# An encoder trunk on one core: the split weight rows laid out without gaps, all at one place modulo 256 bytes from the activations

## The chip, the core and the metric

The kernel runs on one core of a Trainium2 chip. The number compared is the device time of one execution in microseconds (us), the median of several runs. A profiled execution gives the trace from which the rows below are taken. In it TensorE has two rows: PE are the matrix multiplications (MATMUL), PEld the loads of the stationary operand (LDWEIGHTS), one before each MATMUL, loaded while the MATMUL before it still streams. ACT is ScalarE, DVE is VectorE, SP issues most DMAs.

## The reference

A two-layer bidirectional encoder over 256 tokens of width 2048, in float32. Cut to what matters here, it is a row of matrix products with small work between them:

```python
def sq_relu_mlp(h, w1, w2):
    a = jax.nn.relu(h @ w1)
    return (a * a) @ w2

def reference(x, attn_norm, mlp_norm, w_mlp_in, w_mlp_out, even_w_in, even_rpb, even_w_out,
              odd_w_qkv, odd_sink, odd_w_out, final_norm):
    for i in range(DEPTH):
        h = rms_norm(x, attn_norm[i])
        j = i // 2
        if i % 2 == 0:
            x = x + even_mixer(h, even_w_in[j], even_rpb[j], even_w_out[j])
        else:
            x = x + odd_mixer(h, odd_w_qkv[j], odd_sink[j], odd_w_out[j])
        x = x + sq_relu_mlp(rms_norm(x, mlp_norm[i]), w_mlp_in[i], w_mlp_out[i])
    return rms_norm(x, final_norm)
```

`even_mixer` projects to 6144 columns of queries, keys and values, runs 8 heads of neighbourhood attention and 8 of dilated attention and projects back; `odd_mixer` projects to 3072 columns, runs 16 query heads on 4 key heads in a window, and projects back. The MLPs are 2048 to 8192 to 2048. All weights are read once, and the products with them are nearly all of the work.

## The kernel before

**Split products.** To keep float32 accuracy with the one-pass type float32r, each operand is a high part (the value rounded to float32r) and a low part (what the rounding left). A product is high times high, high times low and low times high. The activations lie as `[P, k, 2, T]`: for each group k of 128 input channels, 256 high values and then 256 low values per partition, in the tiles `u` (normed input), `o` (head outputs) and `hid` (MLP hidden layer). The weights come in units of 128 output columns, in halves of eight rows k, 128 x 128 values each. `load_halves` issues the DMA of a half from SP into `r`; `split` (L84, L85) makes the high part `h` on ACT and the low part `l` on DVE. Up to three halves are loaded ahead, from pools of five buffers (`whi`, `wlo`).

**The matrix products.** `k_range` (L155, L157) issues for each k two MATMULs: one with `h` as stationary operand and all 512 columns of the activation's high and low part streamed past it, and one with `l` as stationary operand and the 256 high columns streamed. This document calls these two a *dense pair*. There are 5,344 of them; in the very last unit L152 and L153 take the place of L155, and in the first stage L476 and L477 do the same work as the weights arrive. Pairs of the value projection are other: `value_products` (L276) has the activation `u` stationary and 256 columns of the weight streamed, three MATMULs per k and half of the tokens (`u` high with `h`, `u` high with `l`, `u` low with `h`), 960 in all. Attention adds scores (L312), transposes (L337) and value sums (L356).

**What sets the order.** The program is written out in the order of the units; small work of attention and norms is put between them by a step counter (`later`, `tick`). Each engine runs its own instructions in order.

**Where the operands lie.** In `before` a row of `h` or `l` takes `ROW = P + 8` values, 544 bytes, so that row k begins 32 bytes further modulo 256 than row k-1, and the rows of a half go once round all eight multiples of 32. `h` and `l` of one k lie alike. `u` begins at 128 modulo 256; `hid` and `o` begin at 32; the row of an activation is 2,048 bytes, so all its rows begin alike. The "difference" below is the address of the stationary operand minus that of the streamed one, in bytes modulo 256: in dense pairs it takes all eight multiples of 32 equally often, and every eighth pair has the same one. Weight tiles for the value projection are filled without gaps already, and there the difference between `u` and the streamed weight is 192 in every MATMUL (64 in the first stage, where the rows are 544 bytes apart). In L312 and L356 both operands begin at 32, difference 0.

Of the kernel before, what the change touches and what calls it, by code (L numbers as in the profile page):

```python
# [7 lines left out]
F32 = mybir.dt.float32  # L8
F32R = mybir.dt.float32r
# [5 lines left out]
P = 128  # L15
T = 256
# [8 lines left out]
SCALE = 128.0 ** -0.5  # L25
TW = 384
HALF = KT // 2
ROW = P + 8
RAW_BUFS = 6
LATE = 12  # L30
PART_BUFS = 5
# [11 lines left out]
def encoder(ctx: ExitStack, tc: tile.TileContext, a: dict, outT: bass.AP):  # L43
    nc = tc.nc

    const = ctx.enter_context(tc.tile_pool(name="const", bufs=1))
    raw = ctx.enter_context(tc.tile_pool(name="raw", bufs=RAW_BUFS))
    whi = ctx.enter_context(tc.tile_pool(name="whi", bufs=PART_BUFS))
    wlo = ctx.enter_context(tc.tile_pool(name="wlo", bufs=PART_BUFS))
    held_w = ctx.enter_context(tc.tile_pool(name="held_w", bufs=3))  # L50
    work = ctx.enter_context(tc.tile_pool(name="work", bufs=3))
# [16 lines left out]
    rb2 = const.tile([P, T], F32, name="rb2")  # L68
    rcol = const.tile([P, 2], F32, name="rcol")
    warmed = const.tile([P, 1], F32, name="warmed")  # L70
    gate = const.tile([P, 1], F32, name="gate")

    nc.scalar.dma_start(g, a["gains"])
    nc.vector.memset(ones, 1.0)
# [8 lines left out]
    def split(hi, lo, src):  # L83
        nc.scalar.activation(hi, src, AF.Copy)  # L84
        nc.vector.tensor_sub(lo, src, hi.bitcast(F32))  # L85
# [6 lines left out]
    def need(units, held=0, flat=False):  # L92

        for i, src in enumerate(units):
            pending.extend([(src[:, :HALF, :], HALF, flat),
                            (src[:, HALF:, :], HALF - 2 if i < held else HALF, flat)])

    def load_halves(n):
        while pending and len(loaded) < n:
            src, n, flat = pending.pop(0)  # L100
            r = raw.tile([P, HALF, P], F32, name="r")
            nc.sync.dma_start(r, src)
            h = whi.tile([P, HALF, ROW], F32R, name="h")
            l = wlo.tile([P, HALF, ROW], F32R, name="l")
            if flat:
                h, l = (w.rearrange("p k c -> p (k c)")[:, :HALF * P] for w in (h, l))
                split(h, l, r.rearrange("p k c -> p (k c)"))
                loaded.append((h, l, None))
                continue
            h, l = h[:, :, :P], l[:, :, :P]  # L110
            split(h[:, :n, :], l[:, :n, :], r[:, :n, :])
            tiles = [(h[:, k, :], l[:, k, :]) for k in range(n)]
            if n < HALF:
                h, l = (held_w.tile([P, 2, P], F32R, name=name) for name in ("hh", "hl"))
                split(h, l, r[:, n:, :])
                tiles += [(h[:, k, :], l[:, k, :]) for k in range(2)]
            loaded.append((h, l, tiles))

    def take_half():
        load_halves(AHEAD + 1)  # L120
        return loaded.pop(0)
# [20 lines left out]
    def finish_tasks():  # L142
        while tasks:
            now[0] = max(now[0], tasks[0][0])
            run_due()
# [44 lines left out]
    def gained(k, which, x=None):  # L190
        gk = g[:, which, k:k + 1]
        if x is None:
            x = xs[:, k, :]
        if which == 4:
            nc.scalar.activation(x, x, AF.Copy, scale=gk)
        else:
            nc.scalar.activation(u[:, k, 0, :], x, AF.Copy, scale=gk)
            nc.vector.scalar_tensor_tensor(u[:, k, 1, :], x, gk, u[:, k, 0, :].bitcast(F32),
                                           op0=ALU.mult, op1=ALU.subtract)

    def squares(k, x=None):
        if x is None:
            x = xs[:, k, :]
        if k == 0:
            nc.scalar.activation(ssq, x, AF.Square)
        else:
            sq = work.tile([P, T], F32, name="sq", bufs=2)
            nc.scalar.activation(sq, x, AF.Square)
            nc.vector.tensor_add(ssq, ssq, sq)
# [60 lines left out]
    def value_products(ps, k, h, l):  # L270

        for j in range(2):
            js = slice(j * P, (j + 1) * P)
            out = ps[:, j * T:(j + 1) * T].rearrange("p (a c) -> p a c", a=2)
            for n, (x, y) in enumerate(((0, h), (0, l), (1, h))):
                nc.tensor.matmul(out, u[:, k, x, js], y, start=k == 0 and j == 0 and n == 0,  # L276
                                 stop=k == KT - 1 and n == 2, skip_group_check=True)
# [181 lines left out]
    for k in range(KT):  # L459
        r = raw.tile([P, HALF, P], F32, name="r")  # L460
# [5 lines left out]
    for k in range(KT):  # L466
        r = packs[k]
        x = r[:, :2, :].rearrange("p a c -> p (a c)")
        gained(k, 0, x)
        h, l = (pool.tile([P, HALF, ROW], F32R, name=name)[:, :6, :P] for pool, name in ((whi, "h"), (wlo, "l")))  # L470
        split(h, l, r[:, 2:, :])
        squares(k, x)
        if k == LATE:
            nc.gpsimd.tensor_copy(gate, r[:, 0, 0:1])
        for i in range(4):
            nc.tensor.matmul(sps[i], h[:, i, :], u[:, k].rearrange("p a t -> p (a t)"), start=k == 0, stop=False)  # L476
            nc.tensor.matmul(sps[i][:, :T], l[:, i, :], u[:, k, 0, :], start=False, stop=k == KT - 1)  # L477
        value_products(vps, k, h[:, 4:, :], l[:, 4:, :])
# [5 lines left out]
    with tc.tile_pool(name="attn0", bufs=1) as pool:  # L484
# [25 lines left out]

        q, k, v = [[], []], [[], []], []
        load_halves(1)
        for i in range(2):
            for j, (dst, name, sc) in enumerate(((q, "q", SCALE), (k, "k", 1.0))):
                head_parts(pool, name, 2, sc, dst[i])(sps[2 * i + j])
            load_halves(2)
            attend(pool, o, i, q[i], k[i], v, i, bias_of(i), (LAGS_0[0] + 4 * i,) + LAGS_0[1:])
        norm["waiting"].append(lambda v=v: keep_values(pool, v, vps))
        for p in range(1, 8):
# [6 lines left out]
            q, k, v = [[], []], [[], []], []  # L526
            for i in range(2):
                for j, (dst, name, sc) in enumerate(((q, "q", SCALE), (k, "k", 1.0))):
                    unit(head_parts(pool, name, 2, sc, dst[i]), u)
                h = 2 * p + i  # L530
# [7 lines left out]
    with tc.tile_pool(name="attn1", bufs=1) as pool:  # L538
        o = pool.tile([P, NH, 2, T], F32R, name="o")
        sl = slopes(16)  # L540
        for p in range(2):
            k, v = [[], []], []
# [8 lines left out]
            for i in range(8):  # L551
                h = 8 * p + i
# [3 lines left out]
                       LAGS_1 if h < NH - 3 else LAGS_END, True)  # L556
        project_out(o, 3)
        finish_tasks()
    last_sq = work.tile([P, T], F32, name="last_sq", bufs=1)

    def last_added(ps):
        y = work.tile([P, T], F32, name="y", bufs=1)
# [96 lines left out]
```

## Time and profile before

| | |
|---|---|
| time, median of 3 runs | 2103.64 us (2103.43 to 2104.03) |
| the profiled execution | 2105.7 us, span 2103.8 us |
| granted TensorE clock, mean | 0.996 |
| PE busy | 2086.0 us, 99% of the span |
| DVE busy | 1340.9 us, 64% |
| ACT busy | 1035.6 us, 49% |
| DMA | mean 185 GB/s |

How to read it: a MATMUL's busy time overlaps that of the next (a 512-column one is shown with a mean of 394 ns, but the next begins some 230 ns after it), so the cost of a MATMUL in a full stream is the distance from its start to the next one's start. The chain of waits shows such distances: each of its pieces is how long the chain stayed with a line, with the number of instructions in it. The timeline gives the starts, in us from the start of the span.

### The profile page before, as it was taken

The numbers are of one execution on the slowest core, as the hardware profiler recorded it, in microseconds if no ns is written. First come the engines' busy times: TensorE is split into PE (matmuls) and PEld (weight loads), VectorE is DVE, ScalarE is ACT, GpSimd is POOL, SyncE is SP. The second block draws the span as 40 slices with busy tenths as digits, with TensorE's granted clock in tenths as the row PEclk, the third lists the DMA queues.
The fourth block names the chain that finished last, engine by engine and source line by source line (L and its number), as shares of the span: only waits on it lengthen the run. The fifth ranks groups of instructions, "written<-read, shape, count | busy, mean of one in ns | idle before, by whom it ended". The sixth has DMA issues, their size and how long they took to land.

```text
span 2103.8 us, 31803 instructions
## 1 busy us (share of the span) xinstructions
PE 2086.0 (99%) x12438; PEld 1847.0 (88%) x12438; DVE 1340.9 (64%) x2083; ACT 1035.6 (49%) x1597; POOL 19.1 (1%) x26
## 2 busy tenths in 40 slices
PE   9999999999999999999999999999999999999997
PEld 8999998888888888888889998888888888888886
DVE  7766666766655556665666877766655556665554
ACT  6555555544444444444445655554444444444442
POOL 2100000000000000000000000000000000000000
PEclk9999999999999999999999999999999999999998
DMA  8655555555555555555555444555555555555552
GB/s 301 204 171 169 172 171 177 193 180 190 189 190 189 187 188 190 190 190 190 189 187 186 150 152 150 190 188 188 187 190 189 190 190 190 187 188 189 189 188 91
DMA packets 107174, 388.16 MB, mean 185 GB/s; under 512 B 12128, under 2 KB 12400, under 8 KB 107024
## 3 DMA queue, kind: packets, MB, share of 16 engines
q1 hardware_dynamic: 106128, 383.83, 55.2%
q0 software_dynamic: 752, 2.27, 0.3%
q8 instruction: 97, 1.59, 0.3%
q14 instruction: 53, 0.43, 0.1%
q10 hardware_dynamic: 144, 0.04, 0.0%
HBM read 383.99 MB, written 2.10 MB: 184 GB/s over the span
## 4 chain that ended last, share of the span: by engine, by line
PE 98%; DVE 1%; DMA 0%; ACT 0%; issue 0%; POOL 0%; DVEq 0%; POOLq 0%
PE acc L155 59%; PE acc L157 30%; PE acc L276 5%; PE s_ps L312 1%; PE m_ps L356 1%; PE p_ps L337 1%; DMA tabs<-in_tabs 0%; PE s_ps L476 0%; PE acc L476 0%; DVE xs L576 0%; PE acc L477 0%; DVE l L85 0%; PE acc L152 0%; PE acc L153 0%; PE s_ps L477 0%
## 5 line engine op out<-in xcount | busy, mean ns | idle before, releaser
L85 DVE TENSOR_TENSOR l<-r,h 128x1024 fp32r<-128x1024 f32 (+1 forms) x724 | 881.9, 1218 | 693.5 <-ACT h L84 691.8
L84 ACT ACTIVATE h<-r 128x1024 fp32r<-128x1024 f32 (+1 forms) x724 | 762.2, 1053 | 957.3 <-PE acc L155 632.2
L155 PE MATMUL acc<-u,h 128*128 128x512 f32 x2804 | 983.3, 394 | 0.3 <-DVE z L186 0.3
L157 PE MATMUL acc<-u,l 128*128 128x256 f32 x2804 | 784.0, 280 | 0.0
L155 PE MATMUL acc<-hid,h 128*128 128x512 f32 x2016 | 702.4, 393 | 0.0
L155 PEld LDWEIGHTS acc<-u,h 128*128 128x128 f32 x2804 | 526.7, 188 | 119.1 <-DVE z L186 0.4
L157 PE MATMUL acc<-hid,l 128*128 128x256 f32 x2048 | 572.3, 279 | 0.0
L157 PEld LDWEIGHTS acc<-u,l 128*128 128x128 f32 x2804 | 526.3, 188 | 0.1
L155 PEld LDWEIGHTS acc<-hid,h 128*128 128x128 f32 x2016 | 378.7, 188 | 87.3
L157 PEld LDWEIGHTS acc<-hid,l 128*128 128x128 f32 x2048 | 384.1, 188 | 0.0
L155 PE MATMUL acc<-o,h 128*128 128x512 f32 x500 | 175.2, 394 | 1.1 <-DVE z L186 1.1
L157 PE MATMUL acc<-o,l 128*128 128x256 f32 x500 | 139.8, 280 | 0.0
L276 PE MATMUL acc<-h,u 128*128 128x256 f32 x640 | 121.9, 283 | 0.0
L186 DVE TENSOR_TENSOR z<-acc,t 128x256 f32<-128x256 f32 x273 | 113.4, 417 | 2.1 <-ACT t L184 2.1
L155 PEld LDWEIGHTS acc<-o,h 128*128 128x128 f32 x500 | 93.9, 188 | 22.8 <-DVE z L186 1.7
L276 PEld LDWEIGHTS acc<-h,u 128*128 128x128 f32 x640 | 102.0, 190 | 1.2
L184 ACT ACTIVATE t<-acc 128x256 f32<-128x256 f32 x273 | 99.2, 364 | 4.5 <-PE acc L157 2.7
L157 PEld LDWEIGHTS acc<-o,l 128*128 128x128 f32 x500 | 93.8, 188 | 0.0
L276 PE MATMUL acc<-l,u 128*128 128x256 f32 x320 | 89.9, 281 | 0.0
L276 PEld LDWEIGHTS acc<-l,u 128*128 128x128 f32 x320 | 60.9, 190 | 0.0
L398 DVE SCALAR_TENSOR_TENSOR z<-z 128x256 f32<-128x256 f32 x128 | 54.3, 426 | 4.2
L85 DVE TENSOR_TENSOR hid<-z,hid 128x256 fp32r<-128x256 f32 x128 | 53.4, 419 | 1.3 <-ACT hid L84 1.3
(105 smaller groups left out, 871.0 us busy)
## 6 DMA issues: line engine op xcount, KB each, us to landing
r<-in_w_mlp_in SPq DMA_DIRECT2D x256, 512.0 KB, 4.1
r<-in_w_mlp_out SPq DMA_DIRECT2D x256, 512.0 KB, 4.2
r<-in_even_w_in SPq DMA_DIRECT2D x56, 512.0 KB, 3.6
r<-in_odd_w_qkv SPq DMA_DIRECT2D x40, 512.0 KB, 3.6
r<-in_even_w_out SPq DMA_DIRECT2D x32, 512.0 KB, 3.5
r<-in_odd_w_out SPq DMA_DIRECT2D x32, 512.0 KB, 3.6
r<-in_even_w_v SPq DMA_DIRECT2D x28, 512.0 KB, 3.6
r<-in_start SPq DMA_DIRECT2D x16, 512.0 KB, 4.8
```

Source lines behind the costliest of these rows:

```text
L84: nc.scalar.activation(hi, src, AF.Copy)
L85: nc.vector.tensor_sub(lo, src, hi.bitcast(F32))
L155: nc.tensor.matmul(ps, h, act[:, k].rearrange("p a t -> p (a t)"), start=start, stop=False)
L157: nc.tensor.matmul(ps[:, :T], l, act[:, k, 0, :], start=False, stop=stop)
L184: nc.scalar.activation(t, ps[:, T:], AF.Copy)
L186: nc.vector.tensor_add(z, ps[:, :T], t)
L276: nc.tensor.matmul(out, u[:, k, x, js], y, start=k == 0 and j == 0 and n == 0, stop=k == KT - 1 and n == 2, skip_group_check=True)
L312: nc.tensor.matmul(s_ps[:, i, :], qh[:, x, qs], kh[:, y, :], start=n == 0, stop=n == 2)
L337: nc.tensor.transpose(p_ps[:, j, i * P:(i + 1) * P], s[:, i, j * P:(j + 1) * P], ident)
L356: nc.tensor.matmul(o_ps[:, :T], vv[:, x, j, side * P:(side + 1) * P], pt[:, y, j, :], start=n == 0, stop=n == 5)
L398: nc.vector.scalar_tensor_tensor(z, z, 0.0, z, op0=ALU.max, op1=ALU.mult)
```

## The change

Rows of `h` and `l` lose their gap: `ROW` is gone, a half is `n` rows of 128 values without a space between, and a row's length of 512 bytes makes all rows begin alike modulo 256. `part_rows` builds both tiles: the `h` tile as it is, the `l` tile 64 values longer, with its rows begun `LO_AT = 16` values (64 bytes) into it. The held tiles (rows 6 and 7 of a few halves, put aside) get the same layout. `gate` grows by 32 values, which moves all that is allocated behind it by 128 bytes, and `last_sq` by 56 values, which moves the MLP's pools of the second layer; of both only the old part is used.

In the built program, `h` rows then begin at 64 modulo 256, `l` rows at 128, and `u`, `o` and `hid` at 128. So in every dense pair the difference is 192 for `h` and 0 for `l`. In the value products the stationary `u` stands at difference 64 to a streamed `h` and 0 to a streamed `l`. In L312 and L356 both operands begin at 128, difference 0 as before.

The instructions and their order, with their waits, are the same on every engine; only the address patterns differ, and a split of a half is now one run of values instead of eight with gaps.

```diff
-ROW = P + 8
+
+
+LO_AT = 16
...
-    gate = const.tile([P, 1], F32, name="gate")
+    gate = const.tile([P, 1 + 32], F32, name="gate")
...
+    def part_rows(n, hi_pool=whi, lo_pool=wlo, tag=""):
+        h = hi_pool.tile([P, n, P], F32R, name=tag + "h")
+        l = lo_pool.tile([P, n * P + 64], F32R, name=tag + "l")
+        return h, l[:, LO_AT:LO_AT + n * P].rearrange("p (k c) -> p k c", c=P)
...
-            h = whi.tile([P, HALF, ROW], F32R, name="h")
-            l = wlo.tile([P, HALF, ROW], F32R, name="l")
+            h, l = part_rows(HALF)
             if flat:
-                h, l = (w.rearrange("p k c -> p (k c)")[:, :HALF * P] for w in (h, l))
+                h, l = (w.rearrange("p k c -> p (k c)") for w in (h, l))
...
-            h, l = h[:, :, :P], l[:, :, :P]
...
-                h, l = (held_w.tile([P, 2, P], F32R, name=name) for name in ("hh", "hl"))
+                h, l = part_rows(2, held_w, held_w, "h")
...
-        h, l = (pool.tile([P, HALF, ROW], F32R, name=name)[:, :6, :P] for pool, name in ((whi, "h"), (wlo, "l")))
+        h, l = (w[:, :6, :] for w in part_rows(HALF))
...
-            nc.gpsimd.tensor_copy(gate, r[:, 0, 0:1])
+            nc.gpsimd.tensor_copy(gate[:, 0:1], r[:, 0, 0:1])
...
-    last_sq = work.tile([P, T], F32, name="last_sq", bufs=1)
+    last_sq = work.tile([P, T + 56], F32, name="last_sq", bufs=1)[:, :T]
```

## The prediction

> **What bounds the kernel now.** I read the page first, then the chain of waits, then the timeline of PE. The page:
>
> ```profile
> span 2103.8 us, 31803 instructions
> PE 2086.0 (99%) x12438; PEld 1847.0 (88%) x12438; DVE 1340.9 (64%) x2083; ACT 1035.6 (49%) x1597; POOL 19.1 (1%) x26
> PE 98%; DVE 1%; DMA 0%; ACT 0%; issue 0%; POOL 0%; DVEq 0%; POOLq 0%
> ...
> L85 DVE TENSOR_TENSOR l<-r,h 128x1024 fp32r<-128x1024 f32 (+1 forms) x724 | 881.9, 1218 | 693.5 <-ACT h L84 691.8
> L84 ACT ACTIVATE h<-r 128x1024 fp32r<-128x1024 f32 (+1 forms) x724 | 762.2, 1053 | 957.3 <-PE acc L155 632.2
> L155 PE MATMUL acc<-u,h 128*128 128x512 f32 x2804 | 983.3, 394 | 0.3 <-DVE z L186 0.3
> ...
> L155 PE MATMUL acc<-hid,h 128*128 128x512 f32 x2016 | 702.4, 393 | 0.0
> ...
> L155 PE MATMUL acc<-o,h 128*128 128x512 f32 x500 | 175.2, 394 | 1.1 <-DVE z L186 1.1
> L276 PE MATMUL acc<-h,u 128*128 128x256 f32 x640 | 121.9, 283 | 0.0
> ...
> L276 PE MATMUL acc<-l,u 128*128 128x256 f32 x320 | 89.9, 281 | 0.0
> ```
>
> PE carries 98% of the chain that ended last, and its MATMULs sat idle for about a microsecond in all. What makes the weights waits for PE to free a buffer (ACT 632.2 us at L84), and DVE waits for ACT. So nothing but the distance between the starts of MATMULs decides, and an edit of addresses can act only there. The dense pairs are the 2804, 2016 and 500 above and 24 with held tiles: 5,344. Two starts in the second MLP, 240 pairs apart without another MATMUL between, give the length of one:
>
> ```profile
> 1964.93 0.39 PE L155 MATMUL acc<-hid,h 128*128 128x512 f32 x1
> 1965.15 0.28 PE L157 MATMUL acc<-hid,l 128*128 128x256 f32 x1
> 1965.27 0.39 PE L155 MATMUL acc<-hid,h 128*128 128x512 f32 x1
> 1965.50 0.28 PE L157 MATMUL acc<-hid,l 128*128 128x256 f32 x1
> 1965.62 0.39 PE L155 MATMUL acc<-hid,h 128*128 128x512 f32 x1
> 1965.85 0.28 PE L157 MATMUL acc<-hid,l 128*128 128x256 f32 x1
> 1965.96 0.39 PE L155 MATMUL acc<-hid,h 128*128 128x512 f32 x1
> 1966.19 0.28 PE L157 MATMUL acc<-hid,l 128*128 128x256 f32 x1
> 1966.31 0.40 PE L155 MATMUL acc<-hid,h 128*128 128x512 f32 x1
> 1966.54 0.28 PE L157 MATMUL acc<-hid,l 128*128 128x256 f32 x1
> 1966.66 0.40 PE L155 MATMUL acc<-hid,h 128*128 128x512 f32 x1
> 1966.90 0.28 PE L157 MATMUL acc<-hid,l 128*128 128x256 f32 x1
> 1967.02 0.39 PE L155 MATMUL acc<-hid,h 128*128 128x512 f32 x1
> 1967.24 0.28 PE L157 MATMUL acc<-hid,l 128*128 128x256 f32 x1
> 1967.36 0.40 PE L155 MATMUL acc<-hid,h 128*128 128x512 f32 x1
> 1967.59 0.28 PE L157 MATMUL acc<-hid,l 128*128 128x256 f32 x1
> 1967.71 0.39 PE L155 MATMUL acc<-hid,h 128*128 128x512 f32 x1
> ...
> 2048.53 0.39 PE L155 MATMUL acc<-hid,h 128*128 128x512 f32 x1
> ```
>
> (2048.53 - 1964.93) / 240 = 0.3483 us, so the dense pairs are 5,344 x 0.3483 = 1,861 us, 88% of the span. One nanosecond on each is 5.3 us, a quarter of a per cent.
>
> **Do addresses matter at all?** In these rows the pairs last from start to start 0.34, 0.35, 0.34, 0.35, 0.35, 0.36, 0.34 and 0.35 us, though all do the same: the 512-column MATMUL 0.22 to 0.24 us, the 256-column one 0.11 to 0.13. They stand, from 1964.93, at differences 224, 0, 32, 64, 96, 128, 160, 192, and after eight the row repeats. What changes over eight pairs and then comes back is the difference; the operation, its size and the granted clock are the same. The chain of waits shows a second thing, in the value products, whose difference is 192 throughout:
>
> ```profile
> 114.12 1.36 PE acc L276 x12
> 115.92 5.66 PE acc L276 x48
> ...
> 1214.85 4.09 PE acc L276 x36
> 1219.65 5.66 PE acc L276 x48
> ```
>
> 1.36 / 12 = 113.3 ns and 4.09 / 36 = 113.6 ns, against 5.66 / 48 = 117.9 ns, for the same instructions at the same place: an operation with fixed addresses has **two speeds**, and it keeps the one in which it begins over all of 36 or 48 MATMULs. So at a fixed place the history decides beside the difference. In the dense pairs of before, the difference moves on with each pair and no speed can be kept; their eight pairs average over what the places give.
>
> **A step of 6.67 ns.** The lengths that repeat are whole multiples of one step: 113.3 ns = 17 x 6.67, three of the longer value products 353.7 = 53 x 6.67 (353.3), eight dense pairs 2,786.7 = 418 x 6.67. The starts themselves agree. I took, from the starts to the nanosecond, the 563 starts of L155 at difference 0 that open an undisturbed eight (265 with `u`, 298 with `hid`). Here are the first and last of the 265:
>
> ```profile
> 64.62 0.39 PE L155 MATMUL acc<-u,h 128*128 128x512 f32 x1
> ...
> 1907.81 0.39 PE L155 MATMUL acc<-u,h 128*128 128x512 f32 x1
> ```
>
> Divided by 6.667 ns, with one steady drift of 1.6 millionths taken out, the remainders of each kind lie within 1 ns of one another, over 1,843 us and dozens of interruptions by attention. The distance to the next start depends on that remainder and the difference. So two streams that read SBUF share some rotation of 6.67 ns; that it is an arbitration between the stationary and the streamed reads is my reading and not shown.
>
> **The change, part by part.** *Dense pairs.* All pairs become alike: `h` at 192, `l` at 0. Read off the rows above, the 192 row (1967.36) has 0.23 us for the high and the 0 row (1965.27) 0.12 us for the low MATMUL, 0.35 together: no gain that can be read at 10 ns. But a pair that repeats itself must, if it settles as the value products do, come back at the same remainder: its length is then a multiple of 6.67 ns, 340.0 (51 steps), 346.7 (52) or 353.3 (53), or an alternation of these. 348.3 is 52.25 steps; the nearest that can repeat is 52: 348.3 - 346.7 = 1.67 ns less, x 5,344 = 8.9 us. I take this. The bounds: the fastest halves in the rows, 0.22 + 0.11 = 0.33, give 5,344 x 18 ns = 98 us less; the slowest, 0.24 + 0.13 = 0.37, 116 us more.
>
> *Value products* (960): difference 64 to `h`, 0 to `l` in place of 192. They run at 113.3 or 117.9; if all went from 117.9 to 113.3 ns, 960 x 4.6 = 4.4 us less, and if those at 113.3 went to 117.9, under 1 us more (they are few, a group of 36 and some of 12 like the one above). I take 0. *Scores and value sums* keep difference 0: nothing.
>
> *Splits.* ACT and DVE write runs of 1,024 values without gaps instead of eight runs of 128, as many values in as many instructions. Taken at 0: they stand under PE, with 957 us of idle time on ACT and 693 us on DVE before these groups. Without that cover, a tenth of DVE's 881.9 us would be 88 us; it is covered as long as PE needs more than the 1.22 us that DVE takes for a half, and eight pairs take 2.79. *Larger `gate`, `last_sq` and `l` tiles:* the copies into them are as large as before, 0. *DMAs:* none moved; a faster PE only frees buffers sooner, and DMA has room in this stretch of the second layer:
>
> ```profile
> 1380.00:2080.00 700.00, 700.00 (x4025) 613.15 (x4025) 419.59 (x557) 322.80 (x439) 0.00 (x0) 1.00 0.56 185
> ```
>
> (Its last three numbers are the granted clock, the busy share of DMA, 0.56, and GB/s.) **Sum:** the span 2103.8 - 8.9 = 2094.9; the profiled run took 1.9 us more than its span, and the runs' median, 2103.64, stands 0.2 us below the span, so 2103.6 - 8.9 = 2094.7 us.
>
> **The rivals.** *Faster step:* the pairs settle at 51 steps, 340.0 ns, as the value products do at 113.3: 8.33 x 5,344 = 44.5 us less, 2059 us. For it: three of the eight pairs above read 0.34, and the dense pairs run undisturbed for hundreds of us once they have settled. Against: neither the 192 nor the 0 row is among those that read 0.34.
>
> *Slower step:* they settle at 53 steps, 353.3 ns: 5.0 x 5,344 = 26.7 us more, 2130 us. For it: in the value products the long groups at 117.9 outnumber those at 113.3, and at a fixed place a bad meeting of the two streams is met in each pair instead of in one or two of eight. It decides as soon as a pair exceeds 348.3 by itself.
>
> *Nothing:* the pairs do not settle but wander over the remainders and average what they do now, or the two reads don't meet: 2104 us. The Trainium skill speaks for this one, "SBUF — State Buffer", section "Who interferes with whom": TensorE has two independent read ports, one for the streamed operand and one for LDWEIGHTS, and never waits on anyone. By that, placement is free and the change is worth 0. The two speeds of L276 disagree with it, unless another thing than the reads makes them. "TensorE: Matmul & The Clock Gate", section "Back-to-back issue gap", gives N / 2.4 + 2.5 ns for a warm isolated MATMUL; by it a pair would be an estimated 325 ns, and all of the 23 ns above that, 125 us, would be open to gain. No run here shows a pair that short.
>
> **How the numbers follow.** 52 steps or close by: 0.34. 51 steps or an alternation with it: 0.29; the fixed place can be as good as the best of the old eight, and there are two ways to be faster than 348.3 and one to be slower. Nothing: 0.15. Slower: 0.22. A measurement of this kernel tells 0.2% (4.2 us) from no change; with the first two cases beyond that, faster 0.63, same 0.15, slower 0.22. The time is that of the first, 2094.7, rounded to 2094. The range 2052 to 2116 holds the first three and the milder slower ones; 53 steps lies outside, and so does a pair at the bound of 0.33. The likeliest case's own range is 2090 to 2100 (the value products' 4.4 us to both sides, rounded).
>
> **What would show it.** In the timeline of the second MLP, starts of L155 that are all equally far apart: 0.347 (forecast), 0.340, or 0.353, without the row of eight. A distance that still varies from pair to pair with a mean of 0.348 says that nothing settles. The L276 groups of the chain show by their length over their count which speed they have. If the distances in the second MLP and in attention differ, the interruptions choose the speed. The forecast is wrong if the time moves while the distances don't (then ACT, DVE or DMA became late, to be seen as idle time of PE), or if the pairs are far from any multiple of 6.67 ns.

## The result and the profile after

The change makes the kernel faster: 2066.86 us, the median of four executions (2064.23 to 2068.01), against 2103.84 us before (2103.43 to 2104.60). The ratio is 0.982 (95% interval 0.981 to 0.983). The forecast was 2094 us. The profiled execution of the changed kernel took 2064.23 us, its span is 2062.3 us, 41.5 us shorter than that of before. In it L160 and L162 are the dense pair (L155 and L157 before), L281 the value products (L276), L86 and L87 the split (L84 and L85). The page of after:

```profile
span 2062.3 us, 31803 instructions
PE 2042.2 (99%) x12438; PEld 1825.3 (89%) x12438; DVE 1340.3 (65%) x2083; ACT 1036.9 (50%) x1597; POOL 18.5 (1%) x26
PE 98%; DVE 1%; DMA 0%; ACT 0%; issue 0%; POOL 0%; DVEq 0%; POOLq 0%
...
L87 DVE TENSOR_TENSOR l<-r,h 128x1024 fp32r<-128x1024 f32 (+1 forms) x724 | 881.3, 1217 | 654.2 <-ACT h L86 652.5
L86 ACT ACTIVATE h<-r 128x1024 fp32r<-128x1024 f32 (+1 forms) x724 | 762.4, 1053 | 915.5 <-PE acc L160 604.0
L160 PE MATMUL acc<-u,h 128*128 128x512 f32 x2804 | 960.5, 390 | 0.3 <-DVE z L191 0.3
```

PE still carries 98% of the chain and its MATMULs still sit idle for about a microsecond in all. The splits cost what they did (881.3 and 762.4 us, 881.9 and 762.2 before). So the 41.5 us are in the distances between the starts of MATMULs. The table by stretches counts the 512-column MATMULs of the pairs in two stretches, the first in the first MLP, the second in the second; first of before, then of after. (Its columns: the stretch, its length, busy time and count of PE, the same of PEld, the granted clock, the busy share of DMA and GB/s.)

```profile
415.00:975.00 560.00, 559.48 (x1607) 301.49 (x1606) 1.00 0.58 189
1530.00:1980.00 450.00, 450.00 (x1293) 242.69 (x1292) 1.00 0.57 189
```

```profile
415.00:975.00 560.00, 559.80 (x1647) 308.84 (x1647) 1.00 0.58 193
1530.00:1980.00 450.00, 450.00 (x1325) 248.53 (x1324) 1.00 0.58 194
```

A MATMUL counts when any part of it lies in the stretch, and it is shown 0.39 us long; so a pair lasts (450.00 + 0.39) / 1325 = 339.9 ns, and 348.3 before. The timeline of after shows the same. The first four rows are from the second MLP, and the last is 242 pairs behind the first:

```profile
1699.78 0.39 PE L160 MATMUL acc<-u,h 128*128 128x512 f32 x1
1700.00 0.28 PE L162 MATMUL acc<-u,l 128*128 128x256 f32 x1
1700.12 0.39 PE L160 MATMUL acc<-u,h 128*128 128x512 f32 x1
1700.34 0.28 PE L162 MATMUL acc<-u,l 128*128 128x256 f32 x1
...
1782.06 0.39 PE L160 MATMUL acc<-u,h 128*128 128x512 f32 x1
```

(1782.06 - 1699.78) / 242 = 340.0 ns. From the starts to the nanosecond, all 512 pairs of that stage last 340 ns, the 512-column MATMUL 226 and the 256-column one 114. The row of eight different lengths is gone. One stage stands apart, the last projection out of attention, where 51 pairs lie between these two rows:

```profile
1299.90 0.40 PE L160 MATMUL acc<-o,h 128*128 128x512 f32 x1
...
1317.75 0.40 PE L160 MATMUL acc<-o,h 128*128 128x512 f32 x1
```

17.85 / 51 = 350.0 ns, with the same operands at the same places. By stages, the mean of a pair in ns (only pairs that follow one another directly):

| stage | before | after |
|---|---|---|
| first attention, `u` | 349.1 | 340.8 |
| first projection out, `o` | 348.6 | 340.3 |
| first MLP, its four stages | 348.3 to 348.5 | 340.2, then 340.0 |
| second attention, `u` | 349.7 | 340.3 |
| second projection out, `o` | 348.6 | **348.6** (211 of 246 at 350) |
| second MLP, first stage | 348.5 | 340.8 (39 of 508 at 350) |
| second MLP, the other three | 348.3 | 340.0 |

Over all, a pair went from 348.51 to 340.59 ns: 7.92 x 5,344 = 42.3 us less. A value product went from 117.28 to 118.41 ns: x 864, 1.0 us more (the 96 of the first stage, at 118.5, did not change). Together 41.3 of the 41.5 us.

### The profile page after: what moved, and what is told of

It reads as the page before. It is cut to its first block, busy times and chain, and to the rows that moved or that the text cites. A ratio compares the mean times of both kernels' runs of the same rounds, so it can differ in the third digit from the quotient of the medians.

```text
span 2062.3 us, 31803 instructions
## 1 busy us (share of the span) xinstructions
PE 2042.2 (99%) x12438; PEld 1825.3 (89%) x12438; DVE 1340.3 (65%) x2083; ACT 1036.9 (50%) x1597; POOL 18.5 (1%) x26
## 4 chain that ended last, share of the span: by engine, by line
PE 98%; DVE 1%; DMA 0%; ACT 0%; issue 0%; POOL 0%; DVEq 0%; POOLq 0%
PE acc L160 58%; PE acc L162 30%; PE acc L281 5%; PE s_ps L317 1%; PE m_ps L361 1%; PE p_ps L342 1%; DMA tabs<-in_tabs 0%; PE s_ps L481 0%; PE acc L481 0%; ACT h L86 0%; DVE l L87 0%; DVE xs L581 0%; PE acc L482 0%; PE acc L158 0%; PE acc L157 0%
## 5 line engine op out<-in xcount | busy, mean ns | idle before, releaser
L87 DVE TENSOR_TENSOR l<-r,h 128x1024 fp32r<-128x1024 f32 (+1 forms) x724 | 881.3, 1217 | 654.2 <-ACT h L86 652.5
L86 ACT ACTIVATE h<-r 128x1024 fp32r<-128x1024 f32 (+1 forms) x724 | 762.4, 1053 | 915.5 <-PE acc L160 604.0
L160 PE MATMUL acc<-u,h 128*128 128x512 f32 x2804 | 960.5, 390 | 0.3 <-DVE z L191 0.3
L162 PE MATMUL acc<-u,l 128*128 128x256 f32 x2804 | 774.5, 276 | 0.0
L160 PE MATMUL acc<-hid,h 128*128 128x512 f32 x2016 | 685.6, 389 | 0.0
L160 PEld LDWEIGHTS acc<-u,h 128*128 128x128 f32 x2804 | 526.5, 188 | 107.1 <-DVE z L191 0.4
L162 PE MATMUL acc<-hid,l 128*128 128x256 f32 x2048 | 565.5, 276 | 0.0
L162 PEld LDWEIGHTS acc<-u,l 128*128 128x128 f32 x2804 | 526.5, 188 | 0.1
L160 PEld LDWEIGHTS acc<-hid,h 128*128 128x128 f32 x2016 | 378.4, 188 | 78.5
L162 PEld LDWEIGHTS acc<-hid,l 128*128 128x128 f32 x2048 | 384.5, 188 | 0.0
L160 PE MATMUL acc<-o,h 128*128 128x512 f32 x500 | 173.2, 392 | 1.2 <-DVE z L191 1.2
L162 PE MATMUL acc<-o,l 128*128 128x256 f32 x500 | 139.0, 278 | 0.0
L281 PE MATMUL acc<-h,u 128*128 128x256 f32 x640 | 122.2, 283 | 0.0
L160 PEld LDWEIGHTS acc<-o,h 128*128 128x128 f32 x500 | 93.9, 188 | 21.9 <-DVE z L191 1.9
L281 PEld LDWEIGHTS acc<-h,u 128*128 128x128 f32 x640 | 101.7, 189 | 1.0
L162 PEld LDWEIGHTS acc<-o,l 128*128 128x128 f32 x500 | 93.9, 188 | 0.0
L281 PE MATMUL acc<-l,u 128*128 128x256 f32 x320 | 90.3, 282 | 0.0
L281 PEld LDWEIGHTS acc<-l,u 128*128 128x128 f32 x320 | 60.6, 189 | 0.0
L86 ACT ACTIVATE hid<-z 128x256 fp32r<-128x256 f32 x128 | 51.3, 402 | 6.0 <-DVE z L403 6.0
```

The source lines that it names most:

```text
L160: nc.tensor.matmul(ps, h, act[:, k].rearrange("p a t -> p (a t)"), start=start, stop=False)
L162: nc.tensor.matmul(ps[:, :T], l, act[:, k, 0, :], start=False, stop=stop)
```

## The experiments

Each was timed beside the kernel before on the same chip, which took 2104 to 2105 us in every such group. Where one time is given, it is that of the profiled execution. The first four ask what makes 340 ns: the differences alone, the absolute place, or the rows without gaps.

**All pairs of places, twice.** In the MLPs the place of `h` and `l` changes with every 64 pairs, through the 64 combinations of multiples of 32 bytes. The second kernel goes through them in the opposite order with the two roles exchanged, so that each combination is entered from another neighbour.

```diff
-        h = hi_pool.tile([P, n, P], F32R, name=tag + "h")
+        h = hi_pool.tile([P, n * P + 64], F32R, name=tag + "h")
...
+        ah, al = ((x - 192) % 256 // 4 for x in at)
+        return (h[:, ah:ah + n * P]..., l[:, al:al + n * P]...)
...
+            def at(i, first=128 * layer + 64 * b):
+                n = (first + i) // 4
+                return 32 * (n // 8), 32 * (n % 8)
```

> The changed kernel, but the two differences are set unit by unit in both MLPs: 64 combinations (high part at 0, 32 ... 224, low part at 0, 32 ... 224), each held for four products of 16 pairs, 64 pairs on end; the rest of the kernel stays at 192 and 0, and there is one raw buffer less. Settling (the length of a pair follows from the two differences and from how the stream was entered, and a stretch at one place settles): within each stretch of 64 the pairs become equal after at most some 20, at multiples or half multiples of 6.67 ns, and the combinations differ, from 340 to about 360 ns; 192 and 0 reads 340. Any fixed place (only that the place is fixed matters): all 64 read 340. Rows without gaps alone (dense rows matter, the place doesn't): all 64 read alike. The time is near 2110 us by settling with places good and bad mixed, near 2065 by the other two.

> The same as the first scan with the 64 combinations in another order (the high part changes fastest, and backwards), so each is entered from another neighbour and stands in another layer and stage. Settling with one speed for each place: the two scans agree within 1 ns in each combination. Settling with two speeds, chosen by the entry: most combinations agree, a part (a quarter, as an estimate) reads one of two values 3 to 10 ns apart. If stage or operand (the normed input or the hidden layer) decided instead of the differences, the scans would not agree at all.

Measured: 2101.3 and 2103.9 us. Three combinations of the first kernel in its timeline, by the first and last of a row of undisturbed pairs: `h` 64 and `l` 192 (30 pairs), 192 and 0 (22 pairs), 192 and 32 (28 pairs):

```profile
899.35 0.40 PE L163 MATMUL acc<-u,h 128*128 128x512 f32 x1
...
909.95 0.40 PE L163 MATMUL acc<-u,h 128*128 128x512 f32 x1
...
1735.46 0.40 PE L163 MATMUL acc<-u,h 128*128 128x512 f32 x1
...
1743.16 0.40 PE L163 MATMUL acc<-u,h 128*128 128x512 f32 x1
...
1758.50 0.39 PE L163 MATMUL acc<-u,h 128*128 128x512 f32 x1
...
1768.20 0.39 PE L163 MATMUL acc<-u,h 128*128 128x512 f32 x1
```

10.60 / 30 = 353.3, 7.70 / 22 = 350.0 and 9.70 / 28 = 346.4 ns (346.7 to the nanosecond). The last 40 pairs of each stretch, from the starts to the nanosecond: of 124 readings (62 combinations, each in both kernels), 33 keep within about 1 ns to pairs of 346.7 ns, 19 to 353.3, 7 to 350.0, and most others go round a few lengths with a mean between 346.7 and 353.3. The mean of all is 349.9. In 46 of the 62 combinations the two kernels agree; in the others the same place gives one of two lengths, such as 346.7 and 353.3 at 64 and 160. The shortest is 344.4 ns, at 224 and 0, in both. No reading is 340; the place of the change, 192 and 0, reads 350.0 in both kernels. So a place has settled lengths, often more than one, and which it takes depends on how it is entered. In 52 of the 124 readings every pair has 52 or 53 steps; in none has it 51. But 192 and 0 has 51 in the changed kernel for whole stages and doesn't show it here, so two entries per place are too few to say which other places have a 340.

**Everything 96 bytes further.** One more small tile ahead of `u` moves all activations and weight tiles; the differences stay.

```diff
+    shift = const.tile([P, 24], F32, name="shift")
```

> The changed kernel with an unused tile of 96 bytes ahead of the activations, so that everything of TensorE's in SBUF but the first tile stands 96 bytes further: activations at 224, high parts at 160, low parts at 224 modulo 256, differences 192 and 0 as before. If the differences decide: dense pairs at 340.0 ns, 2062 to 2069 us. If the absolute place decides (a start at 64 or 128 is good in itself): pairs away from 340, 348 on the average or some other settled value, over 2080 us.

Measured: 2064.4 us, a pair of 340.0 ns in the MLPs, and again 350 in 208 of 246 pairs of the last projection. Moved by 96 bytes with the differences kept, the lengths are the same: the place in memory itself is not what decides.

**Gaps between the rows.** The rows stand 768 bytes apart instead of 512, which leaves each difference as it is (with smaller pools, so that it fits).

```diff
-        h = hi_pool.tile([P, n, P], F32R, name=tag + "h")
+        s = P if n == 2 else P + 64
+        h = hi_pool.tile([P, n, s], F32R, name=tag + "h")
```

> The changed kernel with 256 bytes between the rows of each half, so that rows stand 768 bytes apart and still all at differences 192 and 0 (held rows and value tiles stay without gaps); for the space, pools of four buffers in place of five and six. If the place alone decides: dense pairs at 340.0 ns, as in the changed kernel, apart from waits where the smaller pools run short. If rows without gaps are what helps: pairs at about 348 ns and a time of 2100 us or more.

Measured: 2083.4 us, half of the gain. The table by stretches says where:

```profile
415.00:975.00 560.00, 559.61 (x1600) 300.51 (x1599) 1.00 0.57 187
1530.00:1980.00 450.00, 450.00 (x1325) 248.43 (x1324) 1.00 0.59 194
```

The second MLP counts 1325 as after does. The first counts 1600 where after has 1647: 560.39 / 1600 = 350.2 ns. To the nanosecond, 2,005 of its 2,044 pairs last 350.0, and the last projection, at 350 in after, lasts 340.15 here. 2,005 x 10 ns = 20 us, about the whole distance to after. So the lengths that occur are the same with gaps as without, and each stage kept for hundreds of us one of **two lengths, 340.0 or 350.0**, that this place has. That is shown; that the moment at which a stage begins chooses between them, and not the gaps or the smaller pools by themselves, was the next question.

**One MATMUL of another length put in.** In the MLPs, every 32 pairs, one extra MATMUL of N columns, N from 256 to 318 in twos, whose result nobody reads. It moves the starts behind it by a little.

```diff
+    def nudge():
+        n = 256 + 2 * (nudges[0] % 32)
+        nudges[0] += 1
+        ps = aux_ps.tile([P, 512], F32, name="m_ps", bufs=2)
+        nc.tensor.matmul(ps[:, :n], u[:, 0, 0, :P], u[:, 0]...[:, :n], start=True, stop=True)
```

> The changed kernel with 126 extra MATMULs in the MLPs, one ahead of every second product of the first matrix and of each product of the second (32 pairs apart), of 256 to 318 columns, so that the stream of pairs is entered again and again at another phase. Their result is used nowhere; they cost about 0.13 us each, some 16 us. Two settled lengths chosen by the entry (340.0 and 350.0 ns): most stretches of 32 pairs settle at 340, some (5 to 25%) at 350, in stretches that read 340.0 throughout in the changed kernel, and the length of the extra MATMUL modulo 6.67 ns tells which. One settled length, with 350 made by something in the stage of the last projection: no stretch in the MLPs at 350.

Measured: 2089.9 us; the 126 extra MATMULs cost some 17 us themselves. Behind each, within three pairs, the stream settles at 340 or at 350 and keeps it to the next one: 104 times at 340, 21 times at 350. The 350 stands behind the same lengths each time they come round: N = 260, 272, 302 and 318, 288 in three of four times, and 256 when it met a stream at 350. The fourth 288 started some 0.2 us late, because it had to wait for DVE, which was writing `u` (L212); the profile shows no wait before any other of them.

**The map, both ways.** To see whether 350 can be left again, threes of 288, N and N:

```diff
-        n = 256 + 2 * (nudges[0] % 32)
+        n = 288 if nudges[0] % 3 == 0 or nudges[0] >= 96 else 256 + 2 * (nudges[0] // 3)
```

> The same 126 extra MATMULs in the MLPs of the changed kernel, now in threes 32 pairs apart: one of 288 columns, which sent the stream to 350 ns each of the four times that it met it at 340, then one of N, then N again, with N from 256 to 318 in steps of 2. Settling chosen by the entry: N decides, the same way whenever N is alike modulo 16 columns (6.67 ns) or nearly so; after 288 most N bring the stream back to 340 (five of five did by chance before: 258, 262, 274, 290, 304), and a second N from 340 leaves it there except near multiples of 16. If the length drifts between 340 and 350 by what the other engines and DMAs do at that moment: no order in N, and stretches that change without an extra MATMUL.

Measured: 2103.0 us. One three in the timeline (rows of L162 and most of L160 left out):

```profile
1679.04 0.39 PE L160 MATMUL acc<-hid,h 128*128 128x512 f32 x1
1679.38 0.39 PE L160 MATMUL acc<-hid,h 128*128 128x512 f32 x1
1679.72 0.30 PE L172 MATMUL m_ps<-u 128*128 128x288 f32 x1
1679.85 0.39 PE L160 MATMUL acc<-hid,h 128*128 128x512 f32 x1
1680.20 0.40 PE L160 MATMUL acc<-hid,h 128*128 128x512 f32 x1
...
1690.70 0.40 PE L160 MATMUL acc<-hid,h 128*128 128x512 f32 x1
1691.05 0.30 PE L172 MATMUL m_ps<-u 128*128 128x316 f32 x1
1691.19 0.40 PE L160 MATMUL acc<-hid,h 128*128 128x512 f32 x1
...
1692.24 0.39 PE L160 MATMUL acc<-hid,h 128*128 128x512 f32 x1
...
1701.76 0.39 PE L160 MATMUL acc<-hid,h 128*128 128x512 f32 x1
```

Before the first extra MATMUL the pairs are 0.34 us apart. Behind its 288 columns they last (1690.70 - 1680.20) / 30 = 350.0 ns, behind the 316 columns of the second (1701.76 - 1692.24) / 28 = 340.0 ns. Whenever 288 met a stream at 340, it sent it to 350, but for one at 950.74 us, the one that starts late as in the run before. (Behind the first of the kernel, at 409.64 us, the stream was at 350 until a norm interrupted it 3 us later, and at 340 after that.) From 350, every N from 258 on but 272, 288, 302 and 318 led back to 340. A stream at 350 stayed there through the last thirty 288s, 1747 to 2076 us. With N = 268, 282 and 298 the pairs were at 340 at once, from either length. So a single earlier MATMUL is shown to choose between the two lengths, with nothing moved in memory and no other wait. The four lengths that keep 350 are 14 to 16 columns apart, 15.3 on the mean. By the Trainium skill, "TensorE: Matmul & The Clock Gate", section "Back-to-back issue gap", a streamed column costs 1/2.4 ns; 16 columns are then an estimated 6.67 ns, the step of the prediction. The period agrees with that; what turns with it no run shows.

**The places undone in part.** `gate` back at one value moves all that is allocated behind it, the weight tiles, `o` and `hid`, by 128 bytes, while `u`, allocated ahead of it, stays: the pairs with `u` stand at 64 (`h`) and 128 (`l`), those with `o` and `hid` still at 192 and 0.

```diff
-    gate = const.tile([P, 1 + 32], F32, name="gate")
+    gate = const.tile([P, 1], F32, name="gate")
```

> The changed kernel without the 128 bytes behind the gate tile: the differences to the hidden layer and to the head outputs stay 192 and 0 (2528 pairs), those to the normed input become 64 and 128 (2816 pairs). If the differences decide: pairs with the normed input at 350.0 ns (as both scans read 64 and 128), pairs with the others at 340.0 or 350.0; the time is 2064 + 2816 x 10 ns = 2092 us, up to 2117 if the others settle at 350 too. If any fixed place is good: 2064 us.

Measured: 2102.8 us: one small tile holds nearly the whole gain. The pairs with `u` last 350 to 353 ns on the mean of a stage. Those with `hid`, whose place is that of the change, come in two kinds: 350.0 ns in the first `hid` stage of either MLP, 340.0 in the second. One stretch of each, in the first MLP:

```profile
600.00:740.00 140.00, 140.00 (x401) 75.34 (x401) 1.00 0.57 189
960.00:1100.00 140.00, 140.00 (x413) 77.31 (x412) 1.00 0.59 195
```

140.39 / 401 = 350.1 and 140.39 / 413 = 339.9 ns (after has 413 in both). Even the gain of the part that was left in place depends on what ran before it.

**Another fixed place.** All weight rows at differences 64 (`h`) and 192 (`l`) to the activations, one of the places at 353.3 ns in both orders of the scan.

```diff
+    def part_rows(n, hi_pool=whi, lo_pool=wlo, tag="", at=(64, 192)):
```

> The changed kernel with all dense weight rows at the one fixed place 64 and 192 (high part 64, low part 192 from the activations) in place of 192 and 0, one raw buffer less. If the differences decide: pairs at 353.3 ns as in both scans, 2064 + 5344 x 13.3 ns = 2135 us, slower than the kernel before. If a fixed place is what helps: 2064 us.

Measured: 2129.1 us, slower than before by 24.6 us, and the second MLP counts

```profile
1530.00:1980.00 450.00, 450.00 (x1275) 241.15 (x1274) 1.00 0.56 187
```

450.39 / 1275 = 353.3 ns. A place fixed for all pairs is by itself no gain; which place it is decides the sign. (This kernel has one raw buffer less than the change, as the two scans have; so has the kernel of the value products below, and it keeps 340 ns.)

**The high parts fixed, the low parts stepped.** `h` as in the change, `l` rows 544 bytes apart as before.

```diff
-        return h, l[:, LO_AT:LO_AT + n * P].rearrange("p (k c) -> p k c", c=P)
+        return h, l[:, :n * (P + 8)].rearrange("p (k c) -> p k c", c=P + 8)[:, :, :P]
```

> One part of the change alone: rows of the high part without gaps at 192, rows of the low part 544 bytes apart as before (eight differences in turn). If both parts must be fixed for the stream to settle: pairs go round in eights or longer, with a mean between 346 and 352 ns (the scans' row of the high part at 192 has a mean of 349 over the eight low places), 2096 to 2120 us. If the high part's place carries the gain: 340 ns, 2064 us; if it carries half of it: about 344 ns, 2085 us.

Measured: 2117.0 us, slower than before:

```profile
1530.00:1980.00 450.00, 450.00 (x1284) 241.19 (x1283) 1.00 0.56 188
```

450.39 / 1284 = 350.8 ns, and the lengths go on varying. Half of the change loses 12 us; the gain is in both together.

**The value products at other places.** Each pass of the value projection lays its weight at another difference.

```diff
-        need([a["even_w_v"][p, i] for i in range(2)], flat=True)
+        need([a["even_w_v"][p, i] for i in range(2)], flat=True, at=lambda i, p=p: (32 * p - 32, 32 * p - 32))
```

> The changed kernel with the tiles of the nine value projections at nine places (high and low part alike at 0, 32 ... 192 for seven, then 224, and the ninth at 64 and 0), one raw buffer less. The same mechanism in L276: groups settle at different lengths from one place to the next, between 113.3 and 122 ns per MATMUL; the best of them worth at most 960 x 5 ns = 5 us if used throughout. If the value products don't depend on the place: all groups alike at about 118.4 ns. The time stays within 4 us of the changed kernel's.

Measured: 2064.8 us, nothing in the total. The long groups of 36 and 48, in ns for one MATMUL, by the difference between `u` and the streamed weight: 0: 120; 32: 118.3; 64: 113.4; 96: 117.3; 128: 118.6; 160: 120; 192: 117.8; 224: 116.7 to 117.8. At 192, as before, the group of 12 takes 113.45 and the long ones 117.8; at 64 the long ones take 113.4. So here too a place can have two lengths, and 64 is where the long groups come out short in this run; the change has 64 for `h` but 0 for `l`.

**The change again, and a version beyond it.** The change as it is, and one that adds two things: an extra MATMUL of 282 columns near the start of ten stretches (the two projections out and the eight stages of the MLPs), and low value rows moved to where all value products but the 96 of the first stage stand at 64.

```diff
-            h, l = part_rows(HALF)
+            h, l = part_rows(HALF, lo_at=0 if flat else LO_AT)
...
+                    if j == 3:
+                        nudge()
+                    if c == 0:
+                        nudge()
```

> The changed kernel once more, as the yardstick for the next one on the same chip: 2064 to 2068 us, dense pairs at 340.0 ns in the MLPs, and in some stretches of some executions at 350.0, which makes the times spread by a few us (a stretch of 211 pairs at 350 is 2.1 us, one of 500 is 5 us).

> The changed kernel with two additions. Ten extra MATMULs of 282 columns (result unused) at the start of long stretches, one in each output projection and four in each MLP; in the map 282 left the stream at 340.0 from 340 and from 350, at once. And the low rows of the value tiles at 192 like the high ones, so that all value products have difference 64, which ran at 113.4 ns in two of three groups before. Settling by the entry: all stretches of MLPs and output projections at 340.0, which is 2.1 us off the last projection, less 10 x 0.12 us for the extra MATMULs; value products 1 to 4 us less; together 2059 to 2064 us, with less spread than the changed kernel. If the extra MATMULs only helped by chance in the map: times as of the changed kernel or 1 us more.

Measured: the change 2063.92 us (2061.33 to 2064.88; ratio to before 0.981, 0.979 to 0.982), the other 2060.24 us (2059.43 to 2061.18; 0.979, 0.978 to 0.981). The last projection of the second, 46 pairs between these two rows:

```profile
1296.80 0.39 PE L160 MATMUL acc<-o,h 128*128 128x512 f32 x1
...
1312.44 0.39 PE L160 MATMUL acc<-o,h 128*128 128x512 f32 x1
```

and two of its groups of value products in the chain of waits, with the same two of the change after that:

```profile
75.96 5.47 PE acc L286 x48
82.13 4.10 PE acc L286 x36
```

```profile
77.12 5.73 PE acc L281 x48
83.56 4.29 PE acc L281 x36
```

15.64 / 46 = 340.0 ns: the nudge does there what the map said (340.17 over the stage, 348.63 in the change: 246 x 8.46 ns = 2.1 us). The value products fall from 119.3 to 113.9 ns in these groups and from 118.26 to 114.61 over the 864 that were moved: 3.2 us. Ten MATMULs of some 0.12 us cost 1.2 us. The sum, 4.1 us, stands beside 5.4 us in the spans and 3.7 us in the medians; the longest execution of the one, 2061.18, is still shorter than the shortest of the other, 2061.33.

## Why the prediction was right and wrong

**What bounds the kernel: right.** PE's starts decide, ACT, DVE and DMA stayed covered, and the splits cost what they had; "taken at 0" holds.

**That addresses matter: right, and shown.** With the same work in the same order, three sets of fixed places gave 2064, 2103 and 2129 us. The rival *Nothing* falls. A pair takes 340.0 or 353.3 ns by the difference between its two operands. The rule of the Trainium skill that stood for *Nothing* ("SBUF — State Buffer", section "Who interferes with whom", by which TensorE's two read ports are independent and it never waits) doesn't hold here as the prediction used it, as free placement; that it is the two reads that meet, no run shows. The other rule of the Trainium skill ("TensorE: Matmul & The Clock Gate", section "Back-to-back issue gap"), by which a pair could come down to an estimated 325 ns, was not met by any run; 340.0 ns is the shortest settled length there was.

**That pairs at a fixed place settle, and that history chooses: right. That the settled length is a whole multiple of 6.67 ns or an alternation of such: only in part.** 340.0 is 51 steps, 346.7 and 353.3 are 52 and 53. But 350.0 is 52.5 steps, as far from a whole number as can be, and it is no alternation: in the first `hid` stage of the kernel with gaps all 512 pairs last 350 ns alike, 232 for the 512-column MATMUL and 118 for the other. So a pair at this place can come back at half a step, which the prediction ruled out; why, no run shows. It was foreseen that attention's interruptions might choose the speed; that a single instruction can, the map shows.

**The step that failed: "the nearest that can repeat is 52: 348.3 - 346.7 = 1.67 ns less".** The pairs settled at 51, the rival *Faster step*, which had 0.29: 340.59 instead of 346.7 ns on the mean. Where the sum has 8.9 us less for the dense pairs, the traces have 42.3 us less, a gain 33.4 us larger. The value products took 1.0 us where "0" stood and under 1 us was the bound; that bound left out that groups at 117.8 ns could become slower, up to 119.5. And the medians lie closer together than the two profiled executions, by 2.1 us before (2103.6 against 2105.7) and 2.6 us after (2066.9 against 2064.2). 33.4 - 1.0 - 2.1 - 2.6 = 27.7 against 2094.7 - 2066.9 = 27.8 us.

Why it failed: the mean over the old eight places carries no word on where a single one settles. Over the 62 combinations, settled lengths have a mean of 349.9, next to the 348.3 of before, and yet lie between 344.4 and 353.4 (but for two disturbed stretches), and the one that was chosen here has 340.0 as one of its two. That 51 was weighed down because "neither the 192 nor the 0 row is among those that read 0.34" was a wrong use of rows: in before each pair begins at the remainder that the seven other places left, and no pair of its own kind precedes it. The kernel with stepped low rows shows the same from the other side: with `h` at 192 throughout and `l` changing, a pair is 350.8. What could have been worked out from before alone is that 51, 52 and 53 were open; which one, it didn't hold. That the change got 340 in nearly all of its stages is in part luck: with the same differences the kernel with gaps spent 2,005 of the 2,044 pairs of the first MLP at 350 and took 2083.4 us.

**Slower step** was a real case: 353.3 ns and 2129.1 us at 64 and 192, where 2130 was worked out for it. It is what the same edit does with another number.

**What stays open.** What it is that turns in 6.67 ns; why 192 and 0 are a place where 51 steps are possible, and 52.5 too; which other places have 51; and the spread of the timed executions of the change, 2064.2 to 2068.0 us. 3.8 us are 380 pairs at 350 instead of 340, so a stage or two that settles otherwise from one execution to the next would explain it, and the version with nudges spreads over 1.8 us. It was not shown, since only one execution in each set has a trace.

## What to carry to other kernels

When TensorE is never idle and the distance between its instructions still varies with nothing to wait for, look at the addresses of the two operands modulo 256 bytes, and at whether the lengths repeat with the layout. (All of this was measured with float32r operands, and with places in multiples of 32 bytes.) A change of place has to be tried for each place, both operands together, since one fixed place gave 2 per cent less time and another 1 per cent more; the mean of a mixed layout doesn't tell which. And look at each stage on its own: a place can have two lengths, and a stage that fell into the longer one can be moved to the other by a single short instruction at its start.

## What the runs showed of the hardware that was not expected

- A stream of pairs with fixed addresses can have two stable lengths (340.0 and 350.0 ns at 192 and 0), and keeps one for up to 2,000 pairs, until something interrupts it.
- One extra MATMUL decides between them, by its length: 288 columns sent 340 to 350, 282 columns sent 350 to 340, with no wait of any kind.
- The absolute address (shifted by 96 bytes), the spacing of rows (512 or 768 bytes), and which activation is streamed (`u`, `o` or `hid`) made no difference to the lengths that occur; the difference of the two operands modulo 256 did.
- Making one operand's place fixed and leaving the other's stepping was slower (2117.0 us) than stepping both together (2105 us).
